# Weight products of a transformer kernel with tokens stationary: 512 weight columns in one matmul in place of two times 256

## The chip, the cores and the metric

The kernel runs on one core of a Trainium2 chip. The metric is the device time of one execution in microseconds (us). Times of the kernel before are the median of three runs.

## The reference

The program is two transformer blocks on 512 tokens with 1024 channels, all in float32. Every matrix is used once, so nearly all time goes into products of 512 tokens with weights that are streamed from memory.

```python
SEQ, D_MODEL, D_FF = 512, 1024, 2816
# block 1 (conditioned by c: shift, scale and gate of each norm)
u, v, val, gate = jnp.split(h @ w_in + b_in, 4, axis=-1)
y_a = spatial_gating_mixer(gelu(u), gelu(v), ...)      # layer norm of v, causal mixing in chunks of 128
y_b = conformer_conv_mixer(val, gate, ...)             # convolution of width 31
x = x + gate1 * (concat(rmsnorm(y_a), rmsnorm(y_b)) @ w_out)
x = x + gate2 * ((silu(g_ff) * up_ff) @ w_ffn_out)
# block 2, layer 0
proj = h @ w_in                                        # fq, fk, fv (FoX) and nq, kc, vc, ks, ... (NSA)
x = x + rmsnorm(concat(o_fox, o_nsa) @ w_out)
x = x + rmsnorm((silu(h @ w_gate) * (h @ w_up)) @ w_down)
# block 2, layer 1
x = x + rmsnorm(pooled(h) @ w_groups * scale)
x = x + rmsnorm((silu(h @ w_gate) * (h @ w_up)) @ w_down)
```

## The kernel before

**Weights.** `Weights` streams every weight matrix in slabs of at most 512 KB. A slab is loaded into `raw` by the SyncE queue, then split into two exact parts, a head `wh` (ScalarE, `act ... AF.Copy`) and a rest `wl` (VectorE, `subtract`). `W.plan` and `plan_cols(w, k0, kt, c0, n)` list the slabs in the order of use: `kt` blocks of 128 rows by `n` columns, `kt * n` at most 1024. `W.take()` hands out the next slab, and sees to it that `W.look` further ones are split in the program ahead of what follows.

**Products.** Operands are kept as head and rest too, so that each product takes three matmuls: head by head, rest by head, head by rest. There are two forms. In `mm_tile` a weight tile of 128 x 128 is stationary and 512 tokens stream past it. In `mm_tok` a tile of 128 tokens is stationary and weight columns stream past it; its result has the tokens on the partitions. Before the change nearly all products of the second form stream 256 columns (`HS`), and two of them side by side (`e`) fill one PSUM bank `mm` of 512 columns. There are four such banks.

```python
    def mm_tok(o, op, slabs, i, k0=0):
        lst = list(wk(slabs))
        for k, (wh, wl) in enumerate(lst):
            th, tl = op.tok(k0 + k, i)
            TE.matmul(o, lhsT=th, rhs=wh, start=(k == 0), stop=False)
            TE.matmul(o, lhsT=tl, rhs=wh, start=False, stop=False)
            TE.matmul(o, lhsT=th, rhs=wl, start=False, stop=(k == len(lst) - 1))
```

**Where `mm_tok` is used.** The tokens are four tiles `i` of 128.
- The projection `v` of block 1, with vector and Pool work of the convolution behind it (`pump`): two column halves `g`, 8 k blocks, 4 token tiles.
- `fv_step` in the attention of block 2: again 2 x 4 pieces of 8 k blocks. Here the softmax of 24 units (a head and a branch each) runs, and the table `LATER` says behind which unit the next of the deferred projections (`fq_step`, `fk_step`, `fv_step`) is put.
- The output projection of the attention: `geta`, operand `ot`, four column blocks `cb` of 256, 8 k blocks.
- The down projection of the two FFN layers of block 2 (`FfnT`). `front` runs the gate and up products of 17 hidden tiles, then the down projection over the first 16 hidden tiles (`KT0`): for each of four column blocks it takes four slabs at once and goes through them once for every token tile. Then come the other five gate and up pairs, and `last` adds the last 6 hidden tiles for one token half and one half of the columns at a time.

**Order.** The tile framework puts the instructions of each engine in an order of its own, except where `keep` or `Ordered` fix it; each engine then runs its list in that order and waits at semaphores. All operations of VectorE, ScalarE, GpSimd and TensorE pass through one helper, so that the profile calls all of them L113; they are told apart by the names of their tiles.

Of the kernel before, what the change touches and what calls it, by code (L numbers as in the profile page):

```python
# [11 lines left out]
AF = mybir.ActivationFunctionType  # L12
OP = mybir.AluOpType
# [65 lines left out]
LATER = (0, 1, 2, 3, 5, 7, 9, 11, 12, 13, 14, 15, 17, 19)  # L79
# [23 lines left out]
class Ordered:  # L103
    """An engine whose instructions keep the order they are written in while `on` is set."""
# [16 lines left out]
def body(ctx: ExitStack, tc: tile.TileContext, I: dict, out, dbg=None):  # L121
# [64 lines left out]
    def columns(name, w, t=None):  # L186
        """Hands out columns of one tile for small things."""
# [54 lines left out]
    def ada_load(w, c0, n):  # L242
        """Slabs of 4 K blocks for n columns."""
# [12 lines left out]
    def ada_cols(sl, col, bias, bank=MM, one=False):  # L256
        """Columns of silu(c) @ w + b as columns of mod; the K blocks of a slab run in four column groups."""
# [25 lines left out]
    class Weights:  # L283
        """Loads weight slabs ahead of use and splits them into an f32r head and the exact rest."""
# [1457 lines left out]
```

## Time and profile before

| | |
|---|---|
| Runs, us | 1714.64, 1719.37, 1724.15 |
| Median, us | 1719.37 |
| Profiled execution, span from first to last instruction, us | 1714.8 |
| TensorE matmuls (PE) | 1678.9 us busy, 98% of the span, 10489 matmuls |
| TensorE weight loads (PEld) | 1450.7 us, 85%, 10489 |
| VectorE (DVE) | 858.0 us, 50% |
| ScalarE (ACT) | 696.1 us, 41% |
| GpSimd (POOL) | 125.8 us, 7% |
| Mean granted TensorE clock | 0.995 |

Of the profiled execution the profile gives the span alone as its own time; what lies around it is not shown, and the fastest run (1714.64 us) is no longer than it. Busy times are unions: matmuls overlap each other in the pipeline, so the pace of a stream is read from the starts of its matmuls, not from the mean duration of one. The matmuls whose names are `mm<-wh,hid`, `mm<-wl,hid`, `mm<-wh,ot`, `mm<-wh,H` have tokens stationary and weights streaming (the streaming operand is named first); `mm<-hid,wh` and `mm<-H,wh` are the other form.

### The profile page before, as it was taken

What the parts mean: (1) busy time and instruction counts of PE and PEld (TensorE: products, weight loads), DVE (VectorE), ACT (ScalarE), POOL (GpSimd) and SP (SyncE); (2) the same over time, 40 slices, a digit from 0 to 9 for tenths busy, and PEclk for the clock granted to TensorE, in tenths of its full rate; (3) what the DMA queues carried; (4) which work ended last, traced back from release to release, by engine and by line L of the source; (5) the groups of instructions that cost most, each with busy time, mean ns of one, the idle gap of its engine ahead of it and who ended that gap; (6) DMA issues with size and microseconds to landing.
All of it is one profiled execution on the core that took longest, in us unless ns stands there. A gap on an engine that the chain in (4) does not pass through costs nothing.

```text
span 1714.8 us, 25583 instructions
## 1 busy us (share of the span) xinstructions
PE 1678.9 (98%) x10489; PEld 1450.7 (85%) x10489; DVE 858.0 (50%) x1643; ACT 696.1 (41%) x1282; POOL 125.8 (7%) x144
## 2 busy tenths in 40 slices
PE   7998999999999999999999999999999999999998
PEld 4786797777888998877779988899888998889988
DVE  5789672233323584777665433422348734421244
ACT  4586452232222454455557322222237822222222
POOL 0442000000000012000011000000013100000002
PEclk9999999999999999999999999999999999999999
DMA  9648414556233433111035132322433332322511
GB/s 297 161 132 274 135 53 145 151 158 166 74 80 91 124 58 77 48 38 38 26 84 139 50 87 86 99 86 90 125 108 85 87 111 62 88 84 87 148 62 50
DMA packets 276781, 177.65 MB, mean 104 GB/s; under 512 B 20552, under 2 KB 273336, under 8 KB 276664
## 3 DMA queue, kind: packets, MB, share of 16 engines
q1 hardware_dynamic: 272136, 174.89, 35.7%
q10 hardware_dynamic: 4528, 1.12, 0.3%
q8 instruction: 82, 1.34, 0.3%
q14 instruction: 35, 0.29, 0.1%
HBM read 173.90 MB, written 2.10 MB: 103 GB/s over the span
## 4 chain that ended last, share of the span: by engine, by line
PE 50%; DVE 2%; ACT 1%; issue 0%; DVEq 0%; ACTq 0%
PE mm L113 47%; PE ax L113 1%; PE st L113 1%; ACT sq L113 0%; DVE XT L113 0%; DVE pw L113 0%; DVE mg L113 0%; DVE wl L113 0%; ACT H L113 0%; DVE H L113 0%; ACT pw L113 0%; DVE rs L113 0%; ACT wh L113 0%; ACT sd L113 0%; DVE sd L113 0%
## 5 line engine op out<-in xcount | busy, mean ns | idle before, releaser
L113 PE MATMUL mm<-H,wh 128*128 128x512 f32 (+1 forms) x3168 | 871.8, 361 | 2.6 <-ACT H L113 2.3
L113 PEld LDWEIGHTS mm<-H,wh 128*128 128x128 f32 x3168 | 562.6, 189 | 102.0 <-issue 11.8
L113 PE MATMUL mm<-H,wl 128*128 128x512 f32 (+1 forms) x1584 | 568.8, 360 | 0.5 <-DVE wl L113 0.5
L113 DVE TENSOR_TENSOR wl<-raw,wh 128x1024 fp32r<-128x1024 f32 (+1 forms) x257 | 310.4, 1218 | 338.0 <-ACT wh L113 329.3
L113 PEld LDWEIGHTS mm<-H,wl 128*128 128x128 f32 x1584 | 299.5, 189 | 45.3 <-issue 1.5
L113 ACT ACTIVATE wh<-raw 128x1024 fp32r<-128x1024 f32 (+1 forms) x257 | 263.3, 1042 | 146.1 <-PE mm L113 87.6
L113 PE MATMUL mm<-wh,hid 128*128 128x256 f32 x1408 | 254.5, 283 | 0.0
L113 PEld LDWEIGHTS mm<-wh,hid 128*128 128x128 f32 x1408 | 219.8, 192 | 0.7 <-DVE hid L113 0.3
L113 PE MATMUL mm<-wl,hid 128*128 128x256 f32 x704 | 199.2, 284 | 0.1
L113 DVE TENSOR_TENSOR silu<-silu,mm 128x512 f32<-128x512 f32 (+1 forms) x77 | 47.0, 611 | 250.1 <-PE mm L113 245.1
L113 ACT ACTIVATE hid<-silu 128x512 fp32r<-128x512 f32 (+1 forms) x77 | 43.9, 570 | 261.3 <-DVE silu L113 261.2
L113 PEld LDWEIGHTS mm<-wl,hid 128*128 128x128 f32 x704 | 134.9, 192 | 0.3 <-DVE wl L113 0.3
L113 PE MATMUL mm<-hid,wh 128*128 128x512 f32 (+1 forms) x464 | 116.5, 340 | 0.0
L113 PEld LDWEIGHTS mm<-hid,wh 128*128 128x128 f32 x464 | 80.3, 190 | 9.9 <-issue 0.4
L113 PE MATMUL mm<-hid,wl 128*128 128x512 f32 (+1 forms) x232 | 79.0, 341 | 0.0
L113 POOL TENSOR_TENSOR mg<-mg,gb 128x512 f32<-128x512 f32 x32 | 44.2, 1388 | 473.0 <-ACT sq L113 470.0
L113 PE MATMUL mm<-wh,H 128*128 128x256 f32 (+1 forms) x384 | 76.3, 296 | 0.4 <-ACT H L113 0.3
L113 ACT ACTIVATE silu<-silu 128x512 f32<-128x512 f32 (+1 forms) x52 | 29.3, 565 | 114.4 <-DVE silu L113 114.3
L113 DVE TENSOR_TENSOR hid<-silu,hid 128x512 fp32r<-128x512 f32 (+1 forms) x77 | 47.3, 614 | 37.1 <-ACT hid L113 37.1
L113 PEld LDWEIGHTS mm<-wh,H 128*128 128x128 f32 x384 | 62.7, 197 | 2.9 <-issue 1.2
L113 PE MATMUL mm<-wl,H 128*128 128x256 f32 (+1 forms) x192 | 56.6, 295 | 1.8 <-DVE wl L113 1.8
L113 ACT ACTIVATE mg<-mm 128x256 f32<-128x256 f32 (+1 forms) x40 | 15.2, 423 | 101.0 <-PE mm L113 100.9
(268 smaller groups left out, 1715.0 us busy)
## 6 DMA issues: line engine op xcount, KB each, us to landing
adaw<-in_ada_w_dram SPq DMA_DIRECT2D x48, 512.0 KB
raw<-in_w_ffn_in_dram SPq DMA_DIRECT2D x44, 512.0 KB
raw<-in_ffn_w_gate_dram SPq DMA_DIRECT2D x44, 512.0 KB
raw<-in_ffn_w_up_dram SPq DMA_DIRECT2D x44, 512.0 KB
raw<-in_ffn_w_down_dram SPq DMA_DIRECT2D x44, 512.0 KB
raw<-in_w_in_dram SPq DMA_DIRECT2D x16, 512.0 KB
adaw<-in_ada_f_w_dram SPq DMA_DIRECT2D x16, 512.0 KB
raw<-in_attn_w_in_dram SPq DMA_DIRECT2D x16, 512.0 KB
```

Source lines behind the costliest of these rows:

```text
L113: ins = f(*a, **k)
```

## The change

Every `mm_tok` product that streamed 256 columns streams 512. Slabs of these matrices become two k blocks by 512 columns where they were four by 256: the same bytes, the same number of slabs. In `front` the down projection keeps the four token tiles in four PSUM banks at once and takes one slab at a time, passing it once for all four token tiles; before, each group of four slabs was passed by two token tiles a bank. `v` and `fv` are evacuated as 512 columns in one instruction where there were two, one `tensor_reduce` goes, and `LATER` has 10 entries where it had 14. The output projection goes through its k blocks in the order 0, 1, 4, 5, 2, 3, 6, 7. Comments were dropped as well.

```diff
-LATER = (0, 1, 2, 3, 5, 7, 9, 11, 12, 13, 14, 15, 17, 19)
+LATER = (0, 1, 2, 4, 6, 8, 11, 13, 15, 18)
...
-    for g in range(2):
-        for b in range(2):
-            plan_cols(w_in, 4 * b, 4, 512 + g * HS, HS)
+    for b in range(4):
+        plan_cols(w_in, 2 * b, 2, 512, S)
...
             if m == KT0:
-                for cb in range(4):
-                    for k0 in range(0, KT0, 4):
-                        plan_cols(down, k0, 4, cb * HS, HS)
+                for j in range(2):
+                    for k0 in range(0, KT0, 2):
+                        plan_cols(down, k0, 2, j * S, S)
         for j in range(2):
-            for cb in (2 * j, 2 * j + 1):
-                plan_cols(down, KT0, 4, cb * HS, HS)
-            plan_cols(down, KT0 + 4, 2, j * S, S)
+            for k0 in range(KT0, KF, 2):
+                plan_cols(down, k0, 2, j * S, S)
...
-    for g in range(2):
-        sl = [W.take(), W.take()]
-        for i in range(4):
-            pv = MM()
-            mm_tok(pv[:, :HS], hx, sl, i)
-            t = T("vb")
-            tt(t[:, :HS], pv[:, :HS], bvb[:, g * HS:(g + 1) * HS], OP.add)
-            act(vt[i][:, g * HS:(g + 1) * HS], t[:, :HS], AF.Gelu, accum_out=vsum[:, i, g:g + 1])
-            pump(PU[2], PP[2])
-            ada_fetch(NA[1] * (4 * g + i + 1) // 8)
     nmu = C(4)
-    V.tensor_reduce(nmu, vsum, axis=AX.X, op=OP.add)
+    sl = [W.take() for _ in range(4)]
+    for i in range(4):
+        pv = MM()
+        mm_tok(pv, hx, sl, i)
+        t = T("vb")
+        tt(t, pv, bvb, OP.add)
+        act(vt[i], t, AF.Gelu, accum_out=nmu[:, i:i + 1])
+        pump(2 * PU[2], 2 * PP[2])
+        ada_fetch(NA[1] * (i + 1) // 4)
...
             W.look = LD
-            for cb in range(4):
-                sl = [W.take() for _ in range(KT0 // 4)]
-                for b in range(2):
-                    o = MM()
-                    for e in range(2):
-                        mm_tok(o[:, e * HS:(e + 1) * HS], hid, sl, 2 * b + e)
-                    for e in range(2):
-                        act(p.m(2 * b + e, cb // 2)[:, cb % 2 * HS:(cb % 2 + 1) * HS], o[:, e * HS:(e + 1) * HS], AF.Copy)
+            for j in range(2):
+                o = [MM() for _ in range(4)]
+                for s in range(KT0 // 2):
+                    sl = [W.take()]
+                    for i in range(4):
+                        mm_tok(o[i], hid, sl, i, 2 * s, s == 0, s == KT0 // 2 - 1)
+                for i in range(4):
+                    act(p.m(i, j), o[i], AF.Copy)
...
                 o = MM()
-                for e in range(2):
-                    wh, wl, _ = sl[2]
-                    cs = slice(e * HS, (e + 1) * HS)
-                    mm_tok(o[:, cs], self.hid, [sl[e], (wh[:, :, cs], wl[:, :, cs], 2)], i, KT0)
+                mm_tok(o, self.hid, sl, i, KT0)
...
-    def fv_step(g, i):
-        if g not in fvs:
-            fvs[g] = [W.take(), W.take()]
+    def fv_step(i):
+        if i == 0:
+            fvs[0] = [W.take() for _ in range(4)]
         o = MM()
-        mm_tok(o[:, :HS], hu, fvs[g], i)
-        act(fv[i][:, g * HS:(g + 1) * HS], o[:, :HS], AF.Copy)
+        mm_tok(o, hu, fvs[0], i)
+        act(fv[i], o, AF.Copy)
...
-        if p % 2 == 0:
-            later.extend(partial(fv_step, p // 2, i) for i in range(4))
+        if p == 0:
+            later.extend(partial(fv_step, i) for i in range(4))
...
-    geta = lazy(2)
+    geta = lazy(4)
...
-            for e in range(2):
-                mm_tok(o[:, e * HS:(e + 1) * HS], ot, geta(2 * j + e), i)
+            mm_tok(o, ot, geta(j), i, (0, 1, 4, 5, 2, 3, 6, 7))
```

Three places show how the instructions move. First, TensorE at the start of the down projection in `front` of layer 0 (the number behind `mm` is the PSUM bank's tile, behind `wh` and `wl` the slab's). Before:

```order
L113 MATMUL mm_10180<-wh_10030,hid_8837 128x256 x2
L113 MATMUL mm_10180<-wl_10031,hid_8837 128x256
L113 MATMUL mm_10180<-wh_10030,hid_8906 128x256 x2
L113 MATMUL mm_10180<-wl_10031,hid_8906 128x256
L113 MATMUL mm_10180<-wh_10030,hid_8975 128x256 x2
L113 MATMUL mm_10180<-wl_10031,hid_8975 128x256
```

And with the change:

```order
L113 MATMUL mm_9759<-wh_9621,hid_8428 128x512 x2
L113 MATMUL mm_9759<-wl_9622,hid_8428 128x512
L113 MATMUL mm_9759<-wh_9621,hid_8497 128x512 x2
L113 MATMUL mm_9759<-wl_9622,hid_8497 128x512
L113 MATMUL mm_9760<-wh_9621,hid_8428 128x512 x2
L113 MATMUL mm_9760<-wl_9622,hid_8428 128x512
L113 MATMUL mm_9760<-wh_9621,hid_8497 128x512 x2
L113 MATMUL mm_9760<-wl_9622,hid_8497 128x512
L113 MATMUL mm_9761<-wh_9621,hid_8428 128x512 x2
```

One slab now serves two hidden tiles and goes past the banks 9759, 9760, 9761 and 9762 in turn, six matmuls in each, before the next slab is needed; before, a bank stayed in use through four slabs, twice 48 matmuls.

Second, TensorE at the start of `v` in block 1, with the waits (for ScalarE's `wh` and VectorE's `wl`). Before:

```order
L113 MATMUL mm<-wh,H_88 128x256 [waits Activation_49]
L113 MATMUL mm<-wh,H_88 128x256
L113 MATMUL mm<-wl,H_88 128x256 [waits DVE_49]
L113 MATMUL mm<-wh,H_89 128x256 x2
L113 MATMUL mm<-wl,H_89 128x256
L113 MATMUL mm<-wh,H_90 128x256 x2
L113 MATMUL mm<-wl,H_90 128x256
L113 MATMUL mm<-wh,H_91 128x256 x2
L113 MATMUL mm<-wl,H_91 128x256
L113 MATMUL mm<-wh,H_92 128x256 [waits Activation_49]
L113 MATMUL mm<-wh,H_92 128x256
L113 MATMUL mm<-wl,H_92 128x256 [waits DVE_49]
```

And with the change:

```order
L113 MATMUL mm<-wh,H_88 128x512 [waits Activation_49]
L113 MATMUL mm<-wh,H_88 128x512
L113 MATMUL mm<-wl,H_88 128x512 [waits DVE_49]
L113 MATMUL mm<-wh,H_89 128x512 x2
L113 MATMUL mm<-wl,H_89 128x512
L113 MATMUL mm<-wh,H_90 128x512 [waits Activation_49]
L113 MATMUL mm<-wh,H_90 128x512
L113 MATMUL mm<-wl,H_90 128x512 [waits DVE_49]
L113 MATMUL mm<-wh,H_91 128x512 x2
L113 MATMUL mm<-wl,H_91 128x512
L113 MATMUL mm<-wh,H_88 128x512 x2
L113 MATMUL mm<-wl,H_88 128x512
```

The first token tile needed a second slab after four k blocks (H_92); it now needs one after every two (H_90, then H_92 and H_94), and before it goes on to H_92 the order puts a second token tile's products on the first two slabs.

Third, ScalarE in the first units of the attention: `pw` and `sq` are the exponentials of the softmax, `fv` the evacuation of a deferred piece. Before:

```order
L113 ACTIVATE wh<-raw 128x1024
L113 ACTIVATE fv<-mm 128x256 x2
L113 ACTIVATE sq,sm<-sq,mn 128x256
L113 ACTIVATE pw,sm<-pw,mn 128x512
L113 ACTIVATE pw,sm<-pw,mn 128x384
L113 ACTIVATE pw,sm<-pw,mn 128x128
```

And with the change:

```order
L113 ACTIVATE wh<-raw 128x1024 x3
L113 ACTIVATE fv<-mm 128x512 x2
L113 ACTIVATE sq,sm<-sq,mn 128x256
L113 ACTIVATE pw,sm<-pw,mn 128x512
L113 ACTIVATE pw,sm<-pw,mn 128x384
L113 ACTIVATE pw,sm<-pw,mn 128x128
```

The exponentials of the next units stand behind three splits and two whole pieces of `fv`, where they stood behind one split and two half pieces. The order of SyncE's loads has 361 rows before and with the change.

## Rows read from the trace of the kernel before

**Rows 1.** The page: busy time, share of the span and instructions of each engine.

```profile
PE 1678.9 (98%) x10489; PEld 1450.7 (85%) x10489; DVE 858.0 (50%) x1643; ACT 696.1 (41%) x1282; POOL 125.8 (7%) x144
```

**Rows 2.** Waits of PE, longest first: waiter <- releaser, us, times, longest.

```profile
PE ax L113 <- DMA xtok<-in_x_dram: 5.2, 4, 2.4
```

**Rows 3.** Stretches: us, busy us of each engine, PEclk, DMA share, GB/s.

```profile
877.00:934.00 57.00, 56.82 (x456) 53.42 (x455) 31.37 (x65) 36.10 (x84) 9.43 (x7) 1.00 0.53 130
1123.20:1215.40 92.20, 92.20 (x769) 92.15 (x768) 19.49 (x17) 20.81 (x31) 0.00 (x0) 1.00 0.27 84
1271.00:1296.40 25.40, 25.35 (x208) 24.92 (x208) 18.54 (x43) 12.12 (x25) 6.11 (x4) 1.00 0.47 146
1525.00:1619.00 94.00, 94.00 (x777) 93.62 (x777) 20.01 (x18) 22.08 (x33) 0.00 (x0) 1.00 0.29 89
1676.30:1707.20 30.90, 30.90 (x259) 30.84 (x257) 11.95 (x23) 7.51 (x18) 9.05 (x7) 1.00 0.10 35
```

**Rows 4.** PE's groups with shapes apart: xcount | busy us, mean ns | idle.

```profile
L113 PE MATMUL mm<-wh,hid 128*128 128x256 f32 x1408 | 254.5, 283 | 0.0
...
L113 PE MATMUL mm<-hid,wh 128*128 128x512 f32 x240 | 74.2, 390 | 0.0
L113 PE MATMUL mm<-wh,H 128*128 128x256 f32 x320 | 63.3, 296 | 0.4 <-ACT H L113 0.3
...
L113 PE MATMUL mm<-wh,ot 128*128 128x256 f32 x256 | 47.0, 285 | 0.1
```

**Rows 5.** Timeline of PE across the start of a down projection: start us, us, group.

```profile
1079.68 0.62 PE L113 MATMUL mm<-H,wh 128*128 128x512 f32 x2
...
1122.52 0.62 PE L113 MATMUL mm<-H,wh 128*128 128x512 f32 x2
...
1123.20 0.40 PE L113 MATMUL mm<-wh,hid 128*128 128x256 f32 x2
...
1135.44 0.40 PE L113 MATMUL mm<-wh,hid 128*128 128x256 f32 x2
```

**Rows 6.** The four quarters of the attention, six softmax units each (columns of rows 3).

```profile
703.50:750.25 46.75, 46.14 (x297) 38.08 (x296) 36.13 (x126) 24.13 (x66) 2.76 (x4) 0.96 0.21 57
750.25:796.90 46.65, 45.38 (x245) 33.38 (x244) 34.50 (x111) 26.00 (x67) 2.45 (x4) 1.00 0.13 35
796.90:843.20 46.30, 45.71 (x293) 36.05 (x292) 32.52 (x107) 24.66 (x67) 2.45 (x4) 1.00 0.05 12
843.20:885.60 42.40, 41.55 (x243) 29.30 (x241) 32.81 (x111) 24.16 (x65) 2.45 (x4) 1.00 0.12 35
```

**Rows 7.** Waits within the attention (columns of rows 2).

```profile
ACT fv L113 <- PE mm L113: 12.8, 5, 4.9
```

**Rows 8.** Timeline of PE at the start of v, a late slab (columns of rows 5).

```profile
81.70 0.52 PE L113 MATMUL mm<-wl,H 128*128 128x256 f32 x1 [1.79 <-DVE wl L113]
82.02 0.63 PE L113 MATMUL mm<-wh,H 128*128 128x256 f32 x2
...
85.22 0.40 PE L113 MATMUL mm<-wh,H 128*128 128x256 f32 x2
```

**Rows 9.** Timeline of DVE at the start of v (columns of rows 5).

```profile
80.43 1.21 DVE L113 TENSOR_TENSOR wl<-raw,wh 128x1024 fp32r<-128x1024 f32 x1
...
84.82 1.21 DVE L113 TENSOR_TENSOR wl<-raw,wh 128x1024 fp32r<-128x1024 f32 x1
```

**Rows 10.** Timeline of PE behind the last products of layer 0 (columns of rows 5).

```profile
1299.47 0.79 PE L113 MATMUL ax<-bm,xs 128*128 128x128 f32 x5 [1.58 <-ACT xs L113]
```

**Rows 11.** The page's costliest groups: the split of a slab on DVE and ACT.

```profile
L113 DVE TENSOR_TENSOR wl<-raw,wh 128x1024 fp32r<-128x1024 f32 (+1 forms) x257 | 310.4, 1218 | 338.0 <-ACT wh L113 329.3
...
L113 ACT ACTIVATE wh<-raw 128x1024 fp32r<-128x1024 f32 (+1 forms) x257 | 263.3, 1042 | 146.1 <-PE mm L113 87.6
```

**Rows 12.** Timeline of PE in the first products: two banks in turn, three matmuls each.

```profile
49.03 0.62 PE L113 MATMUL mm<-H,wh 128*128 128x512 f32 x2
...
54.49 0.62 PE L113 MATMUL mm<-H,wh 128*128 128x512 f32 x2
```

More of the change, by code (lines that the diff above doesn't have):

```diff
@@ L412, in body @@
         plan_cols(awi, 0, 8, FK + P * p, P)
-        if p % 2 == 0:
-            for b in range(2):
-                plan_cols(awi, 4 * b, 4, FV + p // 2 * HS, HS)
+        if p == 0:
+            for b in range(4):
+                plan_cols(awi, 2 * b, 2, FV, S)
     awo = I["attn_w_out_2"][0]
-    for cb in range(4):
-        cs = slice(cb * HS, (cb + 1) * HS)
-        W.plan([(64 * g, 64 * g + 64, 0, HS, awo[512 + 256 * g:768 + 256 * g, cs].rearrange("(k p) m -> p k m", p=64)) for g in range(2)], 4, HS)
-        plan_cols(awo, 0, 4, cb * HS, HS)
+    for j in range(2):
+        cs = slice(j * S, (j + 1) * S)
+        for b in range(2):
+            W.plan([(64 * g, 64 * g + 64, 0, S, awo[512 + 256 * g + 128 * b:640 + 256 * g + 128 * b, cs].rearrange("(k p) m -> p k m", p=64))
+                    for g in range(2)], 2, S)
+            plan_cols(awo, 2 * b, 2, j * S, S)
     plan_ffn_tok(I["ffn_w_gate_2"][0], I["ffn_w_up_2"][0], I["ffn_w_down_2"][0])
@@ L468, in mm_tile, with mm_tok @@
             op.mm3(o, k0 + k, wh, wl, c0, c1, k == 0, k == len(lst) - 1)
-    def mm_tok(o, op, slabs, i, k0=0):
+    def mm_tok(o, op, slabs, i, k0=0, first=True, last=True):
         lst = list(wk(slabs))
-        for k, (wh, wl) in enumerate(lst):
-            th, tl = op.tok(k0 + k, i)
-            TE.matmul(o, lhsT=th, rhs=wh, start=(k == 0), stop=False)
+        ks_ = k0 if isinstance(k0, tuple) else range(k0, k0 + len(lst))
+        for n, (k, (wh, wl)) in enumerate(zip(ks_, lst)):
+            th, tl = op.tok(k, i)
+            TE.matmul(o, lhsT=th, rhs=wh, start=(first and n == 0), stop=False)
             TE.matmul(o, lhsT=tl, rhs=wh, start=False, stop=False)
-            TE.matmul(o, lhsT=th, rhs=wl, start=False, stop=(k == len(lst) - 1))
+            TE.matmul(o, lhsT=th, rhs=wl, start=False, stop=(last and n == len(lst) - 1))
     def rstd(acc, c0, c1, d, ra=None, out=None, bank=ST):
@@ L816, in body @@
     vt = [vv[i // 2][:, i % 2] for i in range(4)]
-    vsum = C(8).rearrange("p (a b) -> p a b", a=4)
-    for g in range(2):
-        sl = [W.take(), W.take()]
-        for i in range(4):
-            pv = MM()
-            mm_tok(pv[:, :HS], hx, sl, i)
-            t = T("vb")
-            tt(t[:, :HS], pv[:, :HS], bvb[:, g * HS:(g + 1) * HS], OP.add)
-            act(vt[i][:, g * HS:(g + 1) * HS], t[:, :HS], AF.Gelu, accum_out=vsum[:, i, g:g + 1])
-            pump(PU[2], PP[2])
-            ada_fetch(NA[1] * (4 * g + i + 1) // 8)
-    nmu = C(4)
-    V.tensor_reduce(nmu, vsum, axis=AX.X, op=OP.add)
+    nmu = C(4)
+    sl = [W.take() for _ in range(4)]
[7 more added lines that the diff above has]
+        ada_fetch(NA[1] * (i + 1) // 4)
     ts(nmu, nmu, -1.0 / 512, OP.mult)
@@ L1088, in front @@
             W.look = LD
-            for cb in range(4):
-                sl = [W.take() for _ in range(KT0 // 4)]
-                for b in range(2):
-                    o = MM()
-                    for e in range(2):
-                        mm_tok(o[:, e * HS:(e + 1) * HS], hid, sl, 2 * b + e)
-                    for e in range(2):
-                        act(p.m(2 * b + e, cb // 2)[:, cb % 2 * HS:(cb % 2 + 1) * HS], o[:, e * HS:(e + 1) * HS], AF.Copy)
+            for j in range(2):
+                o = [MM() for _ in range(4)]
[5 more added lines that the diff above has]
+                    act(p.m(i, j), o[i], AF.Copy)
             W.look = 4
@@ L1518, in body @@
         later.append(partial(fk_step, p))
-        if p % 2 == 0:
-            later.extend(partial(fv_step, p // 2, i) for i in range(4))
+        if p == 0:
+            later.extend(partial(fv_step, i) for i in range(4))
     gv = gat.rearrange("p i (h b) -> p i h b", b=3)
```

## The prediction

> **What bounds the kernel now.** I read the page first. TensorE (PE) is busy 98% of the span, no other engine over 50% [rows 1]. Then the waits of PE: the longest in total is 5.2 us, for the input at the start [rows 2]. So the kernel is bound by the pace of PE's matmuls almost everywhere, and a change to that pace counts one to one where PE does not wait. Third, the stretches in which the changed products run: in both down projections PE is busy 92.20 of 92.20 us and 94.00 of 94.00, and in the last products of layer 1 30.90 of 30.90, with VectorE (DVE), ScalarE (ACT) and the DMA far below their limits [rows 3]. The busy share doesn't tell the pace, since matmuls overlap: a mean of 283 ns for 256 columns and 390 ns for 512 [rows 4] are times of one matmul through the pipeline. So fourth, the timeline, start to start. From 1079.68 to 1122.52 us there are 63 groups of three matmuls of 512 columns: 0.680 us a group, 226.7 ns a matmul. From 1123.20 to 1135.44 there are 34 groups of three of 256 columns: 0.360 us, 120.0 ns a matmul [rows 5]. Two of 256 cost 240.0 ns where one of 512 costs 226.7: each merged pair is worth 13.3 ns, if a matmul with tokens stationary and 512 weight columns streaming has the pace of one with weights stationary and 512 tokens streaming. The number of weight loads equals that of matmuls [rows 1], so both pay one load of 128 columns each.
>
> **The change part by part.** The work is the same; 2880 matmuls of 256 columns become 1440 of 512. The groups with `wh` count 1408 in the down projections, 256 in the output projection and 320 for `wh,H`, of which `v` and `fv` are 128 each; those with `wl` are half as many again [rows 4]. That is 1056, 192, 96 and 96 pairs. At 13.3 ns the whole is 19.2 us. What of it reaches the end differs by place.
>
> *Down projection, first 16 hidden tiles:* 2 layers x 16 x 3 x 4 token tiles x 2 halves = 768 pairs, 10.2 us, all on PE's path; nothing else there ends a wait [rows 3]. The new order asks for a slab every 4 x 2 x 3 x 0.2267 = 5.44 us, where it was 23.04 us for four (5.76 us each). A split costs 1.04 us on ACT and 1.22 on DVE [rows 11], both idle three quarters of the stretch [rows 3], and two slabs are kept split ahead. Fewer buffers are held too: one slab's two instead of four slabs' eight. All four PSUM banks are open at once, but the first two were read out a pair of gate and up products earlier, and the third is first touched 2.7 us after these end. At the change of the column half the first bank is complete 4.1 us before it is needed again, and one ACT copy empties it. I take the cost of these waits as nothing; the cover is those 2.7 and 4.1 us.
>
> *Last 6 hidden tiles:* 144 pairs a layer, 1.9 us each. In layer 1 PE is saturated up to its last products [rows 3], and what follows the last matmul is unchanged: all 1.9 us counts. In layer 0 a chain over DVE, ACT and POOL comes behind it, for which PE then waits 1.58 us [rows 10]; what PE gains ahead of that wait partly lengthens it. Between nothing and 1.9 us I take the middle, 1.0.
>
> *Output projection:* 192 pairs, 2.6 us. In its stretch PE is busy 56.82 of 57 us, ACT 36.10 [rows 3]. The first column half is free of other work; in the second the residual's chain follows each token tile. I take 1.9 us, all of the first half and half of the second; bounds 1.3 and 2.6.
>
> *v in block 1:* 96 pairs, 1.3 us. DVE is the tight engine here: splits come 4.4 us apart, between the convolution's taps [rows 9], and PE already waits 1.79 us for the second one [rows 8]. With two k blocks to a slab the first token tile meets that same split after 1.8 us of work; the later ones would come late too, but the new order puts a second token tile's work in front of the third slab. The wait stays, the 512-wide evacuations take slightly less of DVE. Between nothing and 1.3 us I take 0.6.
>
> *fv in the attention:* here PE's pace is not the bound. The quarters take 46.75, 46.65, 46.30 and 42.40 us [rows 6]. The deferred pieces in them are, at the paces above, 17.0 us (four half `fv` of 2.88, one projection of 5.44), 16.3, 17.0 and 5.4 us: 11 us less deferred work makes the last quarter only 4 us shorter, 0.36 us for each. With the change they are 21.8, 16.3, 10.9 and 5.4. The first quarter grows by 4.8 x 0.36 = 1.7 us up to the full 4.8, since ACT runs its list in order and already stood 12.8 us behind `fv` pieces [rows 7]; the third shrinks by 6.1 x 0.36 = 2.2 us, at most to the last one's 42.40. So the attention lies between 2.2 us faster and 4.8 slower; I take zero.
>
> **The sum:** 10.2 + 1.9 + 1.0 + 1.9 + 0.6 + 0 = 15.6 us. From the profiled span of 1714.8 us that leads to 1699.2. The median of the runs, 1719.4, is 4.6 us above that span, which is as short as the fastest run; against the median the forecast is 1719.4 - 15.6 = **1703.8 us**, 0.9% faster. A measurement of this kernel can tell about 0.5% (8.6 us) from no change.
>
> **The rivals.** *No cheaper (same).* The trace has no matmul with tokens stationary and 512 columns streaming. If these ran at the pace of two of 256, 240 ns, nothing would be gained: 1719.4 us. For it: the pace is that of the pipeline, not only of the column count. Against it: 512 columns run at the same mean with `hid` streaming as 256 do among each other, 390 and 283 to 296 ns over three operands [rows 4], and the tile loaded is 128 x 128 in both forms. The two paces differ by 106.7 ns for 256 columns, so each matmul carries a fixed 13.3 ns, and the merging removes 1440 of these, if that part is paid for every instruction. The Trainium skill (TensorE: Matmul & The Clock Gate, section Back-to-back issue gap) puts the fixed part of a warm matmul at 2.5 ns; by it the merging would be worth an estimated 3.6 us, and the time 1715.8, again no change to be told. The trace doesn't agree with that page: by its rule 256 columns would start every 109 ns, and here they start every 120.0.
>
> *Attention and early waits eat it (small gain).* The long `fv` pieces hold ACT and PE in the first quarter for the full 4.8 us, the third quarter gives nothing back, and `v`, the second half of the output projection and layer 0's last products give nothing: 10.2 + 1.9 + 1.3 - 4.8 = 8.6 us, 1710.8 us, on the edge of what can be told. For it: the 12.8 us of ACT behind `fv`, and three splits now ahead of it. Against it: the third quarter loses 6.1 us of deferred work.
>
> *Late slabs in the down projection (slower).* The place is each of the 32 slab passes of the two `front` stages. If the next slab's `wl` isn't there, PE stops, and its clock falls. The price stands in the trace: at 81.70 a wait of 1.79 us, behind which five groups of three take 82.02 to 85.22, 3.20 us in place of 1.80 [rows 8]: 3.2 us for a late slab. Five late ones out of 32 cancel the 15.6 us; with eight, one in four, the time is 1719.4 - 15.6 + 25.6 = 1729.4 us. For it: slabs are now taken one at a time, with no reserve but the two ahead. Against it: DVE busy 19.49 us and ACT 20.81 of 92.20, the DMA 0.27 [rows 3], and 5.44 us of work per slab against 2.3 of split. The bank changing with every six matmuls is no cause: in the first products of block 1 two banks alternate every three matmuls, and 8 groups take 49.03 to 54.49 us, 0.68 us each [rows 12]. The Trainium skill (TensorE: Matmul & The Clock Gate, section A second HAM failure mode: psum-queue depth-cycling) tells of a kernel of 512 columns that cycled through banks and whose clock kept falling. In the stretch just named the pace holds, so the trace doesn't bear that out here.
>
> **How the numbers follow.** The forecast, with its own range of 1699 to 1708 from the bounds above: 0.69. More than that, all 19.2 us and a shorter attention: 0.06. Attention and early waits: 0.11, half of it past the 0.5%. No cheaper: 0.08. Late slabs: 0.06. The likeliest case gives 1703.8. The range of 8 in 10 goes from 1697 (19.2 + 2.2 us gained, 1698, and a little for the scatter of runs) to 1711 (the second rival). Faster by over 0.5%: 0.69 + 0.06 + 0.06 = 0.81; within 0.5%: 0.05 + 0.08 = 0.13; slower by over 0.5%: 0.06.
>
> **What would show it.** The count of PE's matmuls falls by 1440 to 9049. In the down projection groups of three start 0.68 us apart, `mm<-wh,hid` has 704 entries, and each `front` stage takes 87.0 us in place of 92.2 with no wait for `wl` at a slab's first pass. The attention's quarters come out uneven, the first about 48 to 51 us. `v` still begins with a wait for `wl` of some 1.8 us. The forecast is wrong if the groups start 0.72 us apart (first rival), if the attention takes over 187 us in place of 182 (second), or if waits of PE for `wl` or half-clock stretches appear inside the down projections (third).

## The result, and the profile after

The changed kernel takes 1692.26 us (median of 4 runs, 1690.45 to 1693.89), the kernel before beside it 1718.38 (4 runs): a ratio of 0.9846, 95% interval 0.9826 to 0.9865. That is 26 us or 1.5% faster; the time lies 11.5 us under the 1703.8 forecast and under the range's 1697. The profiled executions differ by less, 1714.8 and 1692.2 us of span, since before's was a fast one and after's the slowest of its four.

The page's first part answers to [rows 1]: 1440 matmuls fewer, as forecast, and PE still busy 98% of the span.

```profile
PE 1657.5 (98%) x9049; PEld 1375.4 (81%) x9049; DVE 856.6 (51%) x1638; ACT 691.2 (41%) x1254; POOL 128.9 (8%) x144
```

PE's groups with shapes apart answer to [rows 4]: 704 entries of 512 columns where 1408 of 256 were.

```profile
L113 PE MATMUL mm<-wh,hid 128*128 128x512 f32 x704 | 216.8, 389 | 0.0
...
L113 PE MATMUL mm<-wh,ot 128*128 128x512 f32 x128 | 40.9, 396 | 0.0
L113 PE MATMUL mm<-wh,H 128*128 128x512 f32 x128 | 39.6, 393 | 0.0
```

The timeline of PE in the first down projection (start, duration) answers to [rows 5]. From 1195.06 to 1201.18 us there are 9 groups of three: 0.680 us a group, 226.7 ns a matmul, the pace of the other form.

```profile
1195.06 0.62 PE L113 MATMUL mm<-wh,hid 128*128 128x512 f32 x2
...
1201.18 0.62 PE L113 MATMUL mm<-wh,hid 128*128 128x512 f32 x2
```

The changed stretches answer to [rows 3] (us; busy us of PE, PEld, DVE, ACT, POOL; granted clock; DMA share; GB/s): output projection, `front` and last products of layer 0, then of layer 1. PE is busy throughout all five at a clock of 1.00; no late slab, no wait for `wl`.

```profile
872.10:925.60 53.50, 53.50 (x261) 42.37 (x260) 31.36 (x64) 35.20 (x83) 9.43 (x7) 1.00 0.38 109
1114.80:1201.60 86.80, 86.80 (x384) 71.91 (x383) 23.26 (x20) 23.13 (x26) 0.00 (x0) 1.00 0.38 121
1256.30:1280.80 24.50, 24.50 (x109) 20.05 (x108) 18.31 (x44) 11.91 (x23) 5.92 (x4) 1.00 0.43 129
1510.40:1597.20 86.80, 86.80 (x385) 71.87 (x384) 23.26 (x20) 23.25 (x26) 0.00 (x0) 1.00 0.42 126
1651.80:1684.20 32.40, 32.40 (x144) 26.84 (x143) 14.11 (x26) 10.04 (x21) 9.17 (x7) 1.00 0.09 33
```

The four quarters of the attention answer to [rows 6]; here the last is cut where the output projection begins. The third, with 6.1 us less deferred work, is 6.8 us shorter.

```profile
704.70:752.00 47.30, 47.20 (x263) 37.62 (x261) 33.58 (x114) 24.07 (x62) 2.44 (x4) 1.00 0.09 23
752.00:798.20 46.20, 45.88 (x256) 34.56 (x256) 36.64 (x118) 26.24 (x71) 2.45 (x4) 1.00 0.13 35
798.20:837.70 39.50, 38.27 (x212) 27.91 (x210) 29.71 (x100) 22.88 (x59) 2.45 (x4) 1.00 0.13 41
837.70:872.10 34.40, 34.11 (x204) 25.32 (x204) 29.65 (x108) 21.70 (x64) 2.45 (x4) 1.00 0.07 20
```

The unforeseen part is in block 1. At the start of `v` DVE's splits, which were to stay where they were [rows 9], come 3 us earlier, and PE no longer waits for them [rows 8].

```profile
77.44 1.21 DVE L113 TENSOR_TENSOR wl<-raw,wh 128x1024 fp32r<-128x1024 f32 x1
...
81.83 1.20 DVE L113 TENSOR_TENSOR wl<-raw,wh 128x1024 fp32r<-128x1024 f32 x1
```

The 10 us around that wait, before and then after, in the columns of the stretches: PE's busy time goes from 8.30 to 10.00 us, and the granted clock from 0.83 to 1.00.

```profile
80.00:90.00 10.00, 8.30 (x56) 8.30 (x57) 10.00 (x14) 2.94 (x3) 0.00 (x0) 0.83 0.00 0
```

```profile
80.00:90.00 10.00, 10.00 (x46) 8.29 (x45) 9.33 (x14) 2.94 (x3) 0.00 (x0) 1.00 0.00 0
```

By stage, from the starts of the first products in the traces (us): the causal mixing product of block 1 begins at "mixing"; "to down" is from there to block 1's down projection; "attention" from its first scores to the output projection; the others from the first to the last start of their products. Experiments stand below in the same columns.

| kernel | mixing | to down | attention | output | front, each | last, layers 0 and 1 | span |
|---|---|---|---|---|---|---|---|
| before | 135.8 | 274.3 | 173.8 | 56.7 | 92.1 | 26.4, 34.7 | 1714.8 |
| after | 129.5 | 279.8 | 167.4 | 53.4 | 86.8 | 24.5, 32.4 | 1692.2 |
| e1 after, 256 wide | 131.2 | 274.6 | 170.0 | 56.0 | 91.7 | 26.0, 34.1 | 1704.4 |
| e2 attention alone | 135.9 | 273.6 | 170.0 | 56.5 | 92.1 | 26.4, 34.7 | 1710.3 |
| e3 down alone | 130.3 | 273.0 | 172.3 | 56.7 | 86.8 | 24.5, 32.4 | 1694.6 |
| e4 all but attention | 128.8 | 275.2 | 174.6 | 54.0 | 86.8 | 24.5, 32.4 | 1695.2 |
| e5 after, two taps | 135.5 | 280.7 | 167.5 | 53.5 | 86.8 | 24.5, 32.4 | 1698.0 |
| e6 before, four taps | 134.5 | 274.3 | 173.8 | 56.7 | 92.1, 92.6 | 26.4, 34.7 | 1717.4 |
| e7 before, `fv` early | 135.6 | 274.2 | 171.3 | 56.4 | 92.1 | 26.4, 34.7 | 1711.9 |
| e8 after, four taps | 132.1 | 272.3 | 170.6 | 53.5 | 86.8 | 24.5, 32.4 | 1690.5 |
| e9 after, again | 130.0 | 278.9 | 170.6 | 53.5 | 86.8 | 24.5, 32.4 | 1695.4 |
| e11 after, all early | 130.2 | 273.5 | 171.9 | 55.4 | 86.8 | 24.5, 32.4 | 1692.0 |
| e13 after, one number | 131.0 | 278.9 | 171.2 | 53.8 | 86.8 | 24.5, 32.4 | 1699.0 |
| e14 after, three moved | 130.5 | 272.3 | 169.9 | 55.4 | 86.8 | 24.5, 32.4 | 1692.2 |
| e15 after, once more | 129.7 | 278.0 | 170.7 | 53.5 | 86.8 | 24.5, 32.4 | 1695.7 |
| e16 down alone, two taps | 135.8 | 278.6 | 174.5 | 56.7 | 86.8 | 24.5, 32.4 | 1711.6 |
| e17 down alone, again | 130.2 | 271.5 | 172.4 | 56.7 | 86.8 | 24.5, 32.4 | 1691.5 |

### The profile page after: what moved, and what is told of

It is laid out like the page before. It is cut to its first block, busy times and chain, and to the rows that moved or that the text cites. A ratio compares the mean times of both kernels' runs of the same rounds, so it can differ in the third digit from the quotient of the medians.

```text
span 1692.2 us, 22588 instructions
## 1 busy us (share of the span) xinstructions
PE 1657.5 (98%) x9049; PEld 1375.4 (81%) x9049; DVE 856.6 (51%) x1638; ACT 691.2 (41%) x1254; POOL 128.9 (8%) x144
## 4 chain that ended last, share of the span: by engine, by line
PE 91%; DVE 3%; ACT 2%; DMA 2%; SPq 1%; issue 1%; DVEq 0%; ACTq 0%
PE mm L113 83%; PE ax L113 5%; PE st L113 4%; DMA raw<-in_w_ffn_in_dram 1%; DVE wl L113 1%; DMA raw<-in_w_out_dram 1%; SPq L248 0%; ACT wh L113 0%; DMA xtok<-in_x_dram 0%; ACT H L113 0%; ACT sq L113 0%; DVE ax L113 0%; DMA adaw<-in_ada_w_dram 0%; DVE XT L113 0%; DMA raw<-in_ffn_w_up_dram 0%
## 5 line engine op out<-in xcount | busy, mean ns | idle before, releaser
L113 PE MATMUL mm<-wh,hid 128*128 128x512 f32 x704 | 216.8, 389 | 0.0
L113 PEld LDWEIGHTS mm<-wh,hid 128*128 128x128 f32 x704 | 132.0, 188 | 27.3
L113 PE MATMUL mm<-wl,hid 128*128 128x512 f32 x352 | 137.3, 390 | 0.0
L113 PEld LDWEIGHTS mm<-wl,hid 128*128 128x128 f32 x352 | 66.1, 188 | 13.9 <-DVE wl L113 0.3
L113 DVE TENSOR_TENSOR silu<-mm,rsb 128x512 f32<-128x512 f32 (+1 forms) x52 | 31.6, 607 | 76.7 <-PE mm L113 76.6
L113 DVE TENSOR_TENSOR hid<-silu,hid 128x512 fp32r<-128x512 f32 (+1 forms) x77 | 47.3, 614 | 36.4 <-ACT hid L113 36.4
L113 PE MATMUL mm<-wh,H 128*128 128x512 f32 (+2 forms) x256 | 65.3, 344 | 0.2
L113 POOL TENSOR_TENSOR cv<-cv,tap 128x488 f32<-128x488 f32 (+12 forms) x40 | 53.5, 1371 | 89.7 <-ACT cv L113 70.6
L113 ACT ACTIVATE mg<-mm 128x512 f32<-128x512 f32 x24 | 14.3, 597 | 95.4 <-PE mm L113 95.3
```

The lines of the kernel that those rows point to most:

```text
L113: ins = f(*a, **k)
```

## The experiments

**Width and places apart.** e1 keeps the program order and the slabs of the change, but 1344 of its 1440 matmuls run as two of 256 columns.

```diff
-            TE.matmul(o, lhsT=th, rhs=wh, start=(first and n == 0), stop=False)
...
+            for c in range(0, nc_, cw_):
+                TE.matmul(o[:, c:c + cw_], lhsT=t, rhs=w[:, c:c + cw_], start=st, stop=sp)
```

> The changed kernel with its slabs, its order and its table of deferred steps, but every matmul with tokens stationary split into two of 256 columns, except the first and the last of each of the 48 sums (1344 of 1440 are split). Width theory (a fixed 13.3 ns a matmul): down projection groups start 0.72 us apart, the two front stages take 92 us each again in place of 86.8, and the time goes up by about 16 to 18 us, to 1708 to 1710 us. Order theory (one slab at a time past four open banks is what gained): the time stays within 3 us of the changed kernel's 1692.

1708.72 us, ratio 0.9942 (0.9922 to 0.9963): 16.4 over the changed kernel, where 1344 x 13.3 ns make 17.9. The width theory holds. In each `front`, where nothing else moves, 368 split pairs cost 91.7 - 86.8 = 4.9 us, 13.3 ns a pair, at a clock of 1.00:

```profile
1115.00:1206.80 91.80, 91.80 (x753) 91.13 (x752) 23.26 (x20) 23.24 (x26) 0.00 (x0) 1.00 0.36 107
```

The split brings back a weight load with every matmul, so width and number of loads are not told apart here. And 10 us of gain are left with next to no width, most of it in block 1 and the attention.

e2, e3 and e4 take the change's parts: `LATER`, `fv_step` and the plan of `fv` alone; the down projection's plan, `front` and `last` alone; everything but e2's part.

> The kernel before with only fv at 512 columns and the new table LATER. Attention theory (the 6 us of deferred work that leave the third quarter count one to one, the 5 us that enter the first count less than half): 4 to 6 us faster than before, about 1713, the third quarter of the attention 39 to 41 us in place of 46.3. Rival (the attention as a whole gains nothing, its quarters only shift): 1717 to 1719.

> The kernel before with only the down projections changed (1056 pairs). Width theory: 14 us faster, about 1704, both front stages 86.8 to 87.0 us, the quarters of the attention unchanged. Rival (the gain of the change came mostly from other places): less than 8 us.

> The changed kernel with fv at 256 columns and the old table LATER again. Attention theory: 4 to 6 us slower than the changed kernel, about 1697, third quarter 46 us again. Rival (attention gains nothing): 1692 to 1693.

e2: 1713.39 us, 0.9961 (0.9945 to 0.9978), the attention theory's size, its gain in the attention (173.8 to 170.0) and block 1 as before up to the mixing product. e3: 1696.10, 0.9861 (0.9845 to 0.9877), 22.5 us from an edit whose own places give 5.3 + 5.3 + 1.9 + 2.3 = 14.8 by the table. The rest is in block 1, whose code e3 doesn't touch: 5.5 us up to the mixing product, 6.8 up to the down projection; neither its width theory (1704) nor its rival had that. e4: 1698.64, 0.9878 (0.9860 to 0.9895), 6.4 over the changed kernel, a little more than its attention theory said, and in block 1 like e3.

**Why block 1 moved.** In before the convolution's `tap` is a tile with `bufs=2`: ACT writes a scaled row into it, POOL adds it to `cv`. The lists of ACT with what each instruction waits for, before and then after, at the same place:

```
ACTIVATE tap<-glu,fixed 128x487 [waits Pool_49] x2
ACTIVATE wh<-raw 128x1024 [waits DMAHW6_49,DMAHW5_49]
ACTIVATE tap<-glu,fixed 128x486 [waits Pool_49] x2

ACTIVATE tap<-glu,fixed 128x487 x2
ACTIVATE wh<-raw 128x1024 [waits DMAHW6_49,DMAHW4_49]
ACTIVATE tap<-glu,fixed 128x486
ACTIVATE tap<-glu,fixed 128x486 [waits Pool_49]
```

The framework lays all tiles of the program into the memory at once; three taps that waited for POOL wait for nothing with the change. That they landed in other places is argued from this, since the traces hold no addresses. In e3 the order of instructions on all five engines is that of before up to the first `front`; only waits differ, those of loads among them. In e2 order and waits are those of before up to the mixing product, and it begins where it did. The timeline of ACT shows the effect, before and then after (in brackets: idle time before, and what ended it):

```profile
60.85 0.70 ACT L113 ACTIVATE tap<-glu,fixed 128x487 f32<-128x487 f32 x1 [1.20 <-POOL cv L113]
61.47 1.04 ACT L113 ACTIVATE wh<-raw 128x1024 fp32r<-128x1024 f32 x1
...
65.25 0.70 ACT L113 ACTIVATE tap<-glu,fixed 128x485 f32<-128x485 f32 x1 [1.29 <-POOL cv L113]
...
70.05 1.05 ACT L113 ACTIVATE wh<-raw 128x1024 fp32r<-128x1024 f32 x1
```

```profile
59.37 1.28 ACT L113 ACTIVATE tap<-glu,fixed 128x487 f32<-128x487 f32 x2
60.55 1.04 ACT L113 ACTIVATE wh<-raw 128x1024 fp32r<-128x1024 f32 x1
61.50 2.46 ACT L113 ACTIVATE tap<-glu,fixed 128x486 f32<-128x486 f32 x4
...
67.27 1.05 ACT L113 ACTIVATE wh<-raw 128x1024 fp32r<-128x1024 f32 x1
```

The second split on ACT comes 2.8 us earlier, with it DVE's `wl`, and PE's wait of 1.79 us with its half-clock stretch [rows 8] is gone.

e5 gives the changed kernel two fixed tiles for `tap`, so that ACT has to wait as before.

```diff
+    taps, tapn = [tp.tile([P, S], F32, tag=f"tap{i}", name="tap", bufs=1) for i in range(2)], [0]
...
-                t = tp.tile([P, S], F32, tag="tap", name="tap", bufs=2)[:, :c1 - b]
+                t = taps[tapn[0] % 2][:, :c1 - b]
+                tapn[0] += 1
```

> The changed kernel, with the convolution's `tap` in two fixed tiles in turn, so that ACT's third tap and every later one wait for POOL as they do in the kernel before. Nothing of the weight products is touched. Theory A (the 4 to 7 us that block 1 gained came from where the tiles lie, which lets ACT run more taps ahead, so that the splits behind them in its list come 3 to 4 us earlier): PE waits for wl again at the start of v, the causal mixing product starts at about 134 to 136 us in place of 129.5, and the time is 1696 to 1699. Theory B (block 1 gains from the wider products themselves, or from the slab shapes): no change, 1692 to 1693, the mixing product at 129.5.

1699.35 us, 0.9880 (0.9859 to 0.9902), 7.1 more. The mixing product is at 135.5, and PE's timeline has the wait again:

```profile
82.79 0.50 PE L113 MATMUL mm<-wl,H 128*128 128x512 f32 x1 [1.66 <-DVE wl L113]
```

Theory A holds. In the traces of e5 and after every engine runs the same instructions in the same order; up to the mixing product only waits of three taps on ACT, of POOL's additions and of seven loads differ. The clock is not what counts: in e5 it stays at 1.00 from 78 to 136 us, and the product is as late as in before.

e6 and e8 try the reverse, `bufs=4`, on before and on after.

> The kernel before, with four buffers for `tap` in place of two; all weight products are those of before. Theory A: ACT no longer waits for POOL at the third tap, the splits come some 3 us earlier, the wait for wl at 81.7 us and the half-clock stretch behind it go, the mixing product starts at 130 to 132 in place of 135.8, and the time is 1712 to 1715. Theory B: no change, 1718 to 1719.

> The changed kernel with four buffers for `tap`. There ACT already runs five taps ahead before its first wait for POOL. Theory A (the wait for POOL at the first taps was what counted, and it is gone already): 1691 to 1693. If every wait of ACT for POOL counts, the splits come earlier again and it is 1688 to 1690.

e6: 1718.91 us, 0.9988 (0.9975 to 1.0001), no change to be told; theory A missed its size. The framework, told of four buffers, also lists more taps ahead of the splits: the second `wh` comes at 68.94 us, 1.1 earlier than in before, and PE still waits 1.62 for `wl` at `v`. So more buffers alone are no lever; what paid was a list made for two buffers, without the waits at the first three of its taps. e8: 1693.18, as the changed kernel.

**The down projection by itself.** e12 and e16 are e3 with the two fixed taps, e17 is e3 again.

> The kernel before with the new down projection alone, and `tap` in two fixed tiles. Theory A (the down projection itself gives 14 to 15 us, all else that this edit gave, 6 to 8 us, came from block 1's earlier splits): mixing product at 135.5 to 136, front stages 86.8, and 14 to 16 us under the kernel before, about 1704. Theory B (the down projection gives the whole 22 us): 1696 to 1698 as without the two tiles.

> The kernel before with the new down projection alone, and `tap` in two fixed tiles, once more. Theory A: by stage, mixing product at 135 to 136 us as before the change, front stages 86.8 each (5.3 less), last products 24.5 and 32.4 (1.9 and 2.3 less): 14 to 15 us under the kernel before, 1704 to 1705. Theory B: the whole 22 us, 1697.

> The kernel before with the new down projection alone, once more: mixing product at 130 us, 1695 to 1698; 6 to 8 us under e16 by theory A, equal to it by theory B.

e12: ratio 0.9931 (0.9913 to 0.9949), 1707.9 us as the median of six runs (1704.28 to 1713.40); its profiled execution took 2034.48 us at a clock of 0.76 and can't be read by stage. e16: 1710.42, 0.9945 (0.9929 to 0.9962); e17: 1695.71, 0.9868 (0.9852 to 0.9884). By stage theory A holds: 14.8 us less at the changed places in both, and in e16 block 1 has before's wait again, within 0.05 us of its place [rows 8]:

```profile
81.75 0.39 PE L113 MATMUL mm<-wl,H 128*128 128x256 f32 x1 [1.82 <-DVE wl L113]
```

Behind this wait the clock stays at 1.00 in e16 (78 to 105 us), where it was at 0.50 in before: the prediction's price of a late slab, 3.2 us, held 1.4 us of a clock loss that the same wait need not bring.

But e16 keeps only 8 of the 14.8 us, and e17 gains 23: 14.7 us apart, twice what theory A allows. Much of that is the granted clock; e16's profile is of an execution of 1713.37 us (its six take 1705.61 to 1713.37), e17's of one of 1693.20 (its four take 1693.20 to 1698.25). Summed over stretches of 10 us from 30 to 1690 us, (1 - clock) x 10 us comes to 13.6 us in e16, 0.9 in e17, 5.1 in before and 9.8 in after. One of the places lies ahead of the attention and in its first units; e16 and then e17:

```profile
700.00:720.00 20.00, 20.00 (x106) 18.31 (x106) 10.65 (x31) 6.04 (x8) 2.43 (x4) 0.72 0.19 50
```

```profile
700.00:720.00 20.00, 19.43 (x142) 17.04 (x141) 19.59 (x76) 13.43 (x39) 1.22 (x2) 1.00 0.20 52
```

The mean granted clock is known of every run. With (1 - clock) x span taken from each time, an estimate that is too high where PE waits anyway, the medians are 1695.4 us for e12, 1695.0 for e16, 1690.2 for e3, 1688.9 for e17, and 1705.4 to 1707.4 for the kernel before beside them. So the two tiles cost 5 to 6 us, near theory A's 6 to 8, and the down projection alone gains 10 to 12; where the rest of its 14.8 goes is not shown.

**The attention.** e7 puts all eight half pieces of `fv` into the first quarter, 256 wide:

```diff
-LATER = (0, 1, 2, 3, 5, 7, 9, 11, 12, 13, 14, 15, 17, 19)
+LATER = (0, 0, 1, 1, 2, 2, 4, 4, 6, 8, 11, 13, 15, 18)
...
-        if s in LATER:
+        for _ in range(LATER.count(s)):
```

> The kernel before, with all eight half pieces of `fv` put into the first quarter of the attention (23.0 us of deferred work there, then 16.3, 10.9 and 5.4) and still 256 columns wide. Theory A (the distribution makes the gain: deferred work costs one for one in a full quarter and next to nothing in the first): the third quarter takes about 40 us in place of 46.3, the first at most 2 us more, and the time is 1713 to 1715. Theory B (the width of `fv` makes it): 96 pairs x 13.3 ns, 1.3 us at most, 1717 to 1719. Theory C (the rule of 0.36 us for each us of deferred work, both ways): the third quarter 2.2 us shorter, the first 2.1 longer, 1718.5.

1715.99 us, 0.9981 (0.9969 to 0.9993). First and third quarter:

```profile
703.50:754.70 51.20, 50.34 (x360) 44.30 (x359) 35.26 (x119) 25.00 (x67) 2.76 (x4) 0.97 0.12 32
...
800.90:840.30 39.40, 38.17 (x211) 27.91 (x209) 29.66 (x100) 22.70 (x58) 2.45 (x4) 1.00 0.14 41
```

The third is 6.9 us shorter for 6.1 us less deferred work, one for one and a little more; the first 4.4 longer for 6.0 more. Theory A holds for the third quarter; the first takes more than the 2 us it allowed, so that 2.5 us of the attention remain. With `fv` 512 wide too (e2) it is 170.0 against 171.3: 1.3 us, the 96 pairs x 13.3 ns.

e11 puts all ten pieces behind the first ten units, `LATER = (0, 1, ..., 9)`.

> The changed kernel with the ten deferred projections behind the first ten units of the attention (six in the first quarter, four in the second, none later: 32.6, 21.8, 0 and 0 us of deferred work in place of 21.8, 16.3, 10.9 and 5.4). By what the runs so far show, the first quarter grows by about 0.7 us for each us put there and the others change one for one: first +7.6, second +5.5, third -10.9, last -5.4, 3 us faster, 1689. Rival (the first quarter is full by now, one for one there too): no change, 1692. Other rival (ACT's list is held up further): slower than 1694.

1695.93 us, 0.9873 (0.9856 to 0.9889), no gain, and slower than 1694. The quarters take 60.8, 48.8, 31.0 and 31.3 us, the first of them

```profile
697.20:758.00 60.80, 60.80 (x322) 47.08 (x321) 40.56 (x127) 28.75 (x70) 2.44 (x4) 1.00 0.13 35
```

Against after, at the same clock of 1.00, the first is 13.5 us longer for 10.8 us more deferred work, the second 2.6 for 5.5; the third is 8.5 shorter for 10.9 less, the last 3.1 for 5.4. So the first quarter is full by now, the rival's mechanism, and the emptied ones give back less than left them; whether ACT's list holds them up was not settled.

**From the mixing product to block 1's down projection** after took 5.5 us longer than before, e8 2 us less than before.

> The changed kernel once more, for a second profile. In the first one the stretch of block 1 from the causal mixing product to the down projection took 279.8 us, 274.3 in the kernel before. Theory A (scatter of the load waits in that stretch): 272 to 276 us here, and a span of 1686 to 1690. Theory B (the change makes it longer for good; the kernel with two taps showed 280.7): 279 to 281 again, and a span of about 1692.

> The changed kernel with one number of LATER changed, 4 to 3: one piece of `fv` comes a unit earlier in the attention. Nothing that block 1 computes is changed, but the framework then finds other tiles and slightly other orders there, with the waits of SP's loads as in the kernel with the old `fv`. Theory A (the 5 us lost between the mixing product and block 1's down projection hang on that): that stretch takes 273 to 275 us in place of 279, and the time is 4 to 6 us under the changed kernel's of the same batch. Theory B (the wide v costs them): 279 us, no change.

> The changed kernel with LATER as 0, 1, 2, 3, 5, 7, 9, 12, 14, 17: deferred work 27.2, 16.3, 5.4 and 5.4 us or so by quarter, and the waits of SP's loads in block 1 as in the kernel with the old `fv`. Theory A: the stretch behind the mixing product 273 to 275 us, the attention as with the changed kernel (one for one), 4 to 6 us under the changed kernel of this batch. Theory B: no change.

> The changed kernel beside the three others: if the chip alone made the earlier differences, 1692 to 1697, with 279 us behind the mixing product again.

e9 (one run, 1697.18 us) has 278.9 us there, e15 (1695.75, 0.9862, 0.9848 to 0.9877) 278.0: theory B, though the waits are not the same in each. In after a load of `adaw` is late there, and PE's clock falls to 0.66 around it; e15 has that wait too (3.4 us), e9 one of 4.0 us for a slab's `wl`:

```profile
190.70 1.08 PE L113 MATMUL mm<-adaw,fixed 128*32 128x256 f32 x8 [3.31 <-DMA adaw<-in_ada_w_dram]
```

```profile
186.00:196.00 10.00, 6.19 (x43) 3.69 (x33) 2.23 (x7) 3.37 (x5) 0.00 (x0) 0.66 0.94 303
```

e14 (1693.04, 0.9845, 0.9833 to 0.9858) has no such wait and 272.3 us, with the same wide `v`: theory A for the stretch, but the time is only 2.7 us under e15's where it said 4 to 6. e13 (1697.30, 0.9873, 0.9859 to 0.9887) has 278.9, against theory A: the 3.3 us wait is down to 1.2 there, but others are longer. So `v`'s width is not the cause (e8 and e11 have 272.3 and 273.5 us with it), the places and order that the framework finds move this stretch by 7 us, and how was not settled. e14's and e15's intervals overlap: no run beat the changed kernel by more than can be told.

**The fixed part.** e10 splits 256 of the 288 matmuls of the last products into four of 128 columns.

> The changed kernel, with the matmuls of the last 6 hidden tiles split into four of 128 columns: 256 of 288, since the first and the last of each group of 18 stay whole. Theory (every matmul carries a fixed 13.3 ns beside 106.7 for 256 columns): 66.7 ns each, 266.7 for 512 columns in place of 226.7, 256 x 40 ns = 10.2 us more in all, 5.1 in each layer; the last products of layer 1 take 37.5 us in place of 32.4. Rival (the load of the 128 stationary columns bounds a short matmul): more than 66.7 ns each. Other rival (the fixed part is paid per load of new stationary data alone, and halves with the same tokens stationary share it): nearly nothing more.

One run: 1767.01 us. Layer 1's last products take 60.7 us in place of 32.4, at a clock of 1.00:

```profile
1700.53 1.06 PE L113 MATMUL mm<-wh,hid 128*128 128x128 f32 x8
1701.43 0.61 PE L113 MATMUL mm<-wl,hid 128*128 128x128 f32 x4
...
1696.80:1757.40 60.60, 60.60 (x528) 59.87 (x527) 14.98 (x26) 10.04 (x21) 8.94 (x7) 1.00 0.07 27
```

Eight start within 0.90 us: 112 ns each, hardly less than the 120 of 256 columns. A fixed 13.3 ns beside a part in proportion fits 256 and 512 columns, not 128. The first rival, that the load of 128 stationary columns bounds a short matmul, has two more rows for it in the kernel before, both at a clock of 1.00:

```profile
135.84 3.71 PE L113 MATMUL mm<-wsT,vt 128*64 128x128 f32 x64
...
705.64 3.73 PE L113 MATMUL ax<-fixedR,nq 128*128 128x32 f32 x32
```

The 32 of the second row stream only 32 columns past 128 stationary ones, and they too start every 112 ns (3.57 us to the next group). The 64 of the first row have 64 stationary columns and start every 57 ns in the mean (3.65 us to the next). So below 256 columns the pace follows the stationary columns and not the streamed ones. The other rival, that matmuls with the same stationary tokens share the fixed part, fails: four that share them cost 448 ns where one cost 226.7.

## Why the prediction was wrong

The mechanism of the wider matmuls was right and its price too: groups 0.68 us apart, 9049 matmuls, no late slab, none of the three rivals. Two steps beside the down projection failed: that `v`'s wait stays, and that deferred work in the attention counts 0.36 us for each.

- **First 16 hidden tiles**, forecast 10.2: 2 x 5.3 = 10.6 by the table. Right, with the waits counted at nothing.
- **Last 6**, forecast 1.9 and 1.0: 2.3 in layer 1 and 1.9 in layer 0. The chain behind layer 0 did not take half: PE waits for `xs` 1.58 us, as long as before [rows 10].

```profile
1284.42 1.13 PE L113 MATMUL ax<-bm,xs 128*128 128x128 f32 x8 [1.58 <-ACT xs L113]
```

- **Output projection**, forecast 1.9 between 1.3 and 2.6: 3.2, above the whole width's 2.6. With the matmuls split back (e1) 0.7 of it remain, so the order of the k blocks or the slabs may have given something too; the forecast had priced only the width.
- **`v`**, forecast 0.6, "the wait stays": the mechanism failed. The splits were taken as fixed in time. They stood behind ACT's waits for POOL on two tiles, and three of these waits went with the change. Up to the mixing product 6.3 us came instead of 0.6; the two fixed tiles alone (e5) take 6.0 of them back and 7.1 us of the time. In after's profile 5.5 us are lost again in the stretch behind, with the late `adaw` load (3.31 us) and a half clock that costs some 5 us more than in before, so that block 1's net of 0.8 there is close to the forecast by chance; in e8, e11 and e14, with the same wide `v`, that loss does not come.
- **Attention**, forecast 0 by "0.36 us for each": mis-measured. The last quarter was read from 843.20 to 885.60 us, but the output projection begins at 877.33, so that 8.3 us of tail and of the next stage were counted in it. Cut at 877.30, as the other quarters are at the next scores, it reads

```profile
843.20:877.30 34.10, 33.28 (x191) 23.89 (x189) 27.64 (x99) 21.20 (x57) 2.45 (x4) 1.00 0.05 17
```

12.2 us less than the third for 11.6 us less deferred work: one for one was there to be read, and the third quarter's 6.8 us with it. The forecast had put at most 2.2 us there. The first quarter, forecast to grow by 1.7 to 4.8, grew by 0.5 us in after's profile and by 3.9 in e15. Its granted clock was 0.96 in before [rows 6], 1.00 in after and 0.93 in e15:

```profile
704.70:755.30 50.60, 50.50 (x264) 40.28 (x262) 33.84 (x114) 24.12 (x62) 2.44 (x4) 0.93 0.08 22
```

Time times clock makes 44.9, 47.3 and 47.1 us: it grows by some 2.3 us for 4.8 more of deferred work, so that the rate was near for this quarter and wrong for the third. Taken out of the whole attention in the same way, 172.1 us become 167.4 in after, 167.2 in e9 and 167.3 in e15. So the attention gives an estimated 4.7 to 4.9 us where the forecast had none; the 6.4 of after's profile holds 1.7 of before's clock, and the stretch ahead of it loses 1.9, of which 1.7 are clock.

The sum at the profiles, in the order of the list: 10.6 + 2.3 + 1.9 + 3.2 + 6.3 - 5.5 + 6.4 - 1.9 = 23.3 us; the spans differ by 22.6, and the other 0.7 went in the stages between. The range failed with the same two terms: its lower end allowed 1.3 us for `v` and 2.2 for the attention.

Banks changed with every six matmuls throughout both down projections, and the granted clock stayed at 1.00: what the Trainium skill (TensorE: Matmul & The Clock Gate, section A second HAM failure mode: psum-queue depth-cycling) tells of did not come up here. The 1344 pairs split in e1 cost 16.4 us, 12.2 ns each. By the formula for the isolated gap in the Trainium skill (TensorE: Matmul & The Clock Gate, section Back-to-back issue gap) they would be worth an estimated 3.4 us (2.5 ns each), which e1 does not bear out.

## What to carry to other kernels

An edit in a program whose tiles are placed all at once can move time in stages that it doesn't touch: compare not only the order of each engine's list but what each instruction waits for, above all where a buffer handed from one slow engine to another stands ahead of the splits that feed TensorE. A stage's rate is read between equal cuts; a stretch that ends inside the next stage hides it. And price the edit by the stages it touches, then give the rest of the kernel a few us of its own in the range.

## What the runs showed of the hardware

With 128 stationary columns, a matmul of 32 or of 128 streamed columns starts every 112 ns, one of 256 every 120.0, one of 512 every 226.7, all at a clock of 1.00: below 256 columns nearly nothing is saved.

A split on DVE of 1.21 us took 1.74 while POOL worked on `cv` beside it: before, at 71.13 within POOL's taps, and at 76.05 after their end. Of the 13 splits of this size that meet such an addition in the profiles of before and after, 11 take 1.36 to 1.77 us; the 220 in before with POOL idle take 1.23 at most. No run takes POOL's work away, so that this is a coincidence in time and not a cause shown.

```profile
71.13 1.74 DVE L113 TENSOR_TENSOR wl<-raw,wh 128x1024 fp32r<-128x1024 f32 x1 [2.88 <-ACT wh L113]
...
76.05 1.21 DVE L113 TENSOR_TENSOR wl<-raw,wh 128x1024 fp32r<-128x1024 f32 x1
```

The same kernel had its half-clock stretches at other places and for other lengths in its three profiles (after, e9, e15), and the six runs of e16, on one chip, have mean granted clocks from 0.988 to 0.995. From 690 to 720 us, in after's first profile and then in e15, with nothing changed:

```profile
690.00:700.00 10.00, 10.00 (x57) 8.83 (x56) 5.09 (x15) 2.62 (x4) 0.00 (x0) 0.88 0.47 129
700.00:710.00 10.00, 10.00 (x64) 9.01 (x64) 5.27 (x12) 3.50 (x5) 1.83 (x3) 0.94 0.26 71
710.00:720.00 10.00, 10.00 (x48) 8.37 (x47) 9.94 (x33) 6.10 (x13) 0.61 (x1) 1.00 0.15 37
```

```profile
690.00:700.00 10.00, 10.00 (x52) 8.89 (x51) 4.07 (x13) 2.62 (x4) 0.00 (x0) 0.75 0.28 69
700.00:710.00 10.00, 10.00 (x58) 8.98 (x56) 4.41 (x8) 3.33 (x5) 1.83 (x3) 0.84 0.25 67
710.00:720.00 10.00, 10.00 (x39) 8.35 (x39) 8.82 (x31) 6.09 (x13) 0.61 (x1) 0.73 0.16 40
```

1.8 us of clock are lost there in the one and 6.8 in the other (10 us times one minus the clock, summed): stages are compared between kernels only where their clock agrees, or over several profiles.
